# Moving the loads and splits of the token sums at sample's changes of stage, and starting sample's groups of heads later, in an encoder layer on one core

## The chip, the cores and the metric

The kernel runs on one core of a Trainium2 chip. The metric is the device time of one execution in microseconds (us). Three runs of the kernel before took 2102.96, 2103.63 and 2103.91 us, median 2103.63. A profile was taken of one more execution.

## The reference

Two sequences, prompt (512 tokens) and sample (1024 tokens), both 2048 wide, go through the same encoder layer:

```python
def mixer_layer(x, ...):
    h = rms_norm(x, norm_g)
    z = h @ w_in
    c_val, c_glu, c_gate, q, k, v, a_gate = jnp.split(z, split_points, axis=-1)
    q, k = apply_rope(q), apply_rope(k)
    conv_out = conformer_conv(c_val, c_glu, w_dw, b_dw, ln_g, ln_b, w_pw) * silu(c_gate)
    attn_out = banded_sink_attention(q, k, v, sink) * silu(a_gate)
    return x + concatenate([conv_out, attn_out]) @ w_out
```

`conformer_conv` is a gated linear unit, a depthwise convolution over 31 tokens, a layer norm and a product with `w_pw`. The attention has 8 heads in 2 groups (4 query heads share one key and value head), works in blocks of 128 tokens and looks one block to either side. A final RMS norm follows. Everything is in 32-bit floats.

## The kernel before

**Products.** Each 32-bit operand is split into an upper and a lower part (`parts`, lines 496 and 497: ACT makes the upper part, DVE subtracts for the lower; lines 499 and 500 do the same with a norm's factor; line 404 and 406 for the weights of prompt's jobs), and three matmuls (upper × upper, upper × lower, lower × upper) stand for one. The product of sample's tokens with `w_in` is done in the manner of Strassen and Winograd: a `Unit` (from line 93) makes a 2 × 2 block of the output from seven products instead of eight. Each of the seven (`product`, matmuls on line 199) is 12 matmuls of 128x128 by 128x512, 84 in a unit. Its operands are seven sums of weight tiles (`make0` to `make3`, line 141 subtracts) and seven sums of token tiles. When a product is done, `tap` (line 225, ACT) copies its PSUM bank out, and DVE adds it in (line 245). P1, P6, P7 and P4 share bank a, P5 and P3 bank c, P2 has b, so the next product of a bank waits for the tap.

**Token sums.** The seven sums of a half of the depth (in the order A11, A12, S2, S1, S3, S4, A22) stay in SBUF as split tiles (pool T1, 28 tiles, just seven sums of four tiles) for a whole stage. Four of them were computed once and written to memory (`sum_S`), the other three are plain tiles of the tokens (`xT_s`). `load_sum` (line 838, DMA issue on line 853) fetches one sum of four tiles on the queue of SP: steps 0 and 3 into the p tiles, the others into two A tiles (pool A has 4, p has 4). `token_sum` (line 777) splits them.

**Stages.** Sample's product runs in four stages: a plain block and 7 units, then 8 units for the convolution's channels on the other half of the depth, then 14 and 14 for the rest. The first two units of the second and fourth stage run interleaved, as a side pair. Between stages the token sums change; `switch` (line 1878, called at lines 1905 and 1906 for sample and a third time for the later product with `w_out`) hangs loads and splits onto the products of the last unit of the old stage and the first of the new: the loads of steps 0, 1 and 2 go ahead of the last unit, and after product n of it the sum of step n − 1 is split and the sum of step n + 2 loaded, since a sum is no longer needed once its product is done.

**After that.** 44 jobs of 48 matmuls (line 645) multiply prompt's tokens with `w_in`, 16 jobs with `w_pw` follow (line 337 and 1781 are plain products too), then units (`Onto`) for the product with `w_out` of both sequences, whose results DVE adds from PSUM (line 292).

**The order of the work.** The matmuls' order is written out by hand. Beside them run lanes (`Lane`, line 63), queues of generators for the small work: `conv` (depthwise convolution, lines 976, 1005 and 1013; L1039 to L1042 and L949 make the rotated and gated parts), `prep` (sums and norms: the squares of sample's rows are on line 873, a small chain of DVE turns them into factors, L712 puts them on diagonals and the matmul of L717 spreads them), and `attn` (attention). With every three matmuls a lane earns 3 × 216 ns times its rate, and a generator that yields a cost pauses until that much has been earned. So a cost of `rate * 4000` is 4 us of matmul time. `attend` (in `encoder`) puts the two groups of sample's heads into the lane `attn` at the start of prompt's jobs, with rate 1.8. `group` (line 1087) loads keys, values and the first queries, waits, splits them, and then does block by block `attention` (line 1112): scores (L1129), mask, maximum and sum (L1132), exponentials (L1143), transposes (L1163) and the product with the values (L1158).

The place in the program is not yet the place on an engine. A scheduler puts the instructions of every engine in order, by readiness and priority; an instruction that is ready, and whose tile is free, can be ahead of others that the program has before it. DMAs are issued by SP (its queue has most loads and stores) and a few by POOL.

Of the kernel before, what the change touches and what calls it, by code (L numbers as in the profile page):

```python
# [720 lines left out]
class Sequence:  # L721
# [365 lines left out]
    def group(self, g):  # L1087

        e, nc = self.e, self.e.nc
        if self.s == 0:  # L1090
            k, v = ([e.T1([self.T]) for _ in range(2)] for _ in range(2))
        else:
            kv = e.F([2, self.T], F32R), e.F([2, self.T], F32R)
            k, v = [(t[:, 0], t[:, 1]) for t in kv]
        held = []
        for src in (self.k_d[g], self.v_d[g]):
            held.append(e.A([self.T], F32))
            nc.sync.dma_start(held[-1], src)
        self.load_query(g, 0)
        yield e.attn.rate * LEAD  # L1100
        for dst in (k, v):
            e.parts(dst[0], dst[1], held.pop(0))
            yield 3500
        for b in range(self.B):
            yield from self.attention(g, b, k, v)

# [697 lines left out]
def encoder(ctx, tc, a):  # L1804
    e = Encoder(ctx, tc, a)
    sample, prompt = Sequence(e, 0), Sequence(e, 1)
# [9 lines left out]
    stages = [  # L1816
        [plain] + [u(0, False) for u in conv[1:]],
        [u(1, True) for u in conv],
        [u(1, False) for u in rest],
        [u(0, True) for u in rest],  # L1820
    ]
# [53 lines left out]
        u.order = TURNS  # L1875
    plain.before.append(first)

    def switch(unit, nxt, g, seq):

        held = {}  # L1880

        roomy = seq is sample

        def load(step):
            held[step] = seq.load_sum(SUMS[ALONE[step]], g, step % 3 or roomy and step == 6)

        def follow(step):
            for j, x in enumerate(held.pop(step)):
                seq.token_sum(SUMS[ALONE[step]], g, j, x)
            if step < 4 - roomy:  # L1890
                load(step + 3)
            elif step == 4 and roomy:
                load(6)

        def begin():
            load(0)
            load(1)
            load(2)

        unit.before.append(begin)  # L1900
        for step in range(7):
            u, at = (unit, step + 1) if step < 6 else (nxt, 0)
            u.after.setdefault(at, []).append(lambda step=step: follow(step))

    switch(stages[0][-1], stages[1][0], 1, sample)
    switch(stages[2][-1], stages[3][0], 0, sample)

    def pace(unit, rate, lane=e.conv):
        unit.before.append(lambda: setattr(lane, "rate", rate))
# [70 lines left out]
    def prepare():  # L1980
        until(lambda: sample.convolved == NC, e.conv)
        for half in halves:
            e.prep.add(half.prepare())
        e.prep.add(halves[0].fetch())
        e.attn.add(mix.attention_sums())
        for group in prompt.groups:
            e.attn.add(group)
# [29 lines left out]
    over[0][0].after[3] = [lambda: mix.put(6)]  # L2017
    over[0][-1].before += [e.prep.drain, e.attn.drain]
    switch(over[0][-1], over[1][0], 0, mix)

    def norm_last():
# [25 lines left out]
    at = len(e.preps)  # L2047
# [58 lines left out]
```

## Time and profile before

| | |
|---|---|
| median of three runs | 2103.63 us |
| profiled execution | 2106.77 us |
| its span in the profile | 2104.9 us |
| TensorE (PE) busy | 2067.4 us, 9250 matmuls |
| VectorE (DVE) busy | 1751.4 us |
| ScalarE (ACT) busy | 1042.5 us |
| DMA | 494.53 MB, 235 GB/s on average |

A row of the timeline has the start in us, the duration, engine, line (L199 is line 199 of the kernel before), operation, written and read tile, shape and count; in brackets the idle time of the engine ahead of it and what ended that. In the list of waits stand the matmul that waited, the instruction that released it, the total in us, the number of such waits and the longest. In the table by windows stand start and end, length, then busy time and count of PE, PEld (weights loaded into the array), DVE, ACT and POOL, then the granted clock of TensorE as a share of full speed, the share of the DMA engines in use, and GB/s. Matmuls overlap a little, so a run of them is read from the starts: 24 of 128x512 take 5.44 us, 0.2267 each.

### The profile page before, as it was taken

To read this page: it belongs to the slowest core of one execution; us is meant where nothing else is said; L and a number is where in the kernel's file an instruction comes from. 1 tells how busy PE (TensorE), PEld (TensorE's weight loads), DVE (VectorE), ACT (ScalarE), POOL (GpSimd) and SP (SyncE) were. 2 spreads that over 40 slices of the span, in tenths; PEclk is the share of its full clock that TensorE was granted. 3 is DMA by queue.
4 is the path that set the end of the run, shared out by engine and by line. 5 is a ranking of instruction groups with operands and counts; after the bars stand their busy time and mean duration, and the time that the engine had idled before them with its cause. 6 is when DMAs were issued, how large, how long until landed. Compare 5 with 4: busy or idle time off the path is not lost. (4 is left out here: it accounts for less than half of the span.)

```text
span 2104.9 us, 26942 instructions
## 1 busy us (share of the span) xinstructions
PE 2067.4 (98%) x9250; PEld 1696.0 (81%) x9250; DVE 1751.4 (83%) x2851; ACT 1042.5 (50%) x1685; POOL 77.3 (4%) x92
## 2 busy tenths in 40 slices
PE   9999999999999999999999999999999999999997
PEld 7878888888877887778888888887878788888886
DVE  8758798998889999999556877776799988898876
ACT  6476435333454443544456777336553343455444
POOL 0001110000002111100000000000000000000000
PEclk9999999999999999999999999999999999999999
DMA  7988887865577776955456565996689898678998
GB/s 265 322 290 247 203 217 226 295 201 172 181 228 193 172 170 170 270 162 163 156 170 190 169 187 180 315 332 223 233 276 305 269 321 295 207 251 272 299 323 276
DMA packets 247449, 494.53 MB, mean 235 GB/s; under 512 B 23184, under 2 KB 83984, under 8 KB 247312
## 3 DMA queue, kind: packets, MB, share of 16 engines
q1 hardware_dynamic: 234640, 469.74, 67.4%
q0 software_dynamic: 12672, 23.07, 6.9%
q8 instruction: 72, 1.18, 0.2%
q14 instruction: 65, 0.53, 0.1%
HBM read 331.77 MB, written 160.96 MB: 234 GB/s over the span
## 5 line engine op out<-in xcount | busy, mean ns | idle before, releaser
L199 PE MATMUL a<-t,hl 128*128 128x512 f32 x2640 | 633.4, 390 | 10.0 <-ACT u L225 4.8
L199 PEld LDWEIGHTS a<-t,hl 128*128 128x128 f32 x2640 | 493.2, 188 | 118.4 <-ACT u L225 8.1
L496 ACT ACTIVATE hl<-raw 128x1024 fp32r<-128x1024 f32 (+3 forms) x360 | 324.6, 902 | 435.6 <-DVE raw L141 96.3
L497 DVE TENSOR_TENSOR hl<-raw,hl 128x1024 fp32r<-128x1024 f32 (+3 forms) x360 | 370.1, 1028 | 152.6 <-ACT hl L496 148.7
L645 PE MATMUL a<-t,hl 128*128 128x512 f32 x1344 | 329.4, 395 | 0.5 <-DVE hl L497 0.5
L199 PE MATMUL c<-t,hl 128*128 128x512 f32 x1320 | 320.1, 390 | 3.1 <-DVE u L292 2.0
L199 PEld LDWEIGHTS c<-t,hl 128*128 128x128 f32 x1320 | 247.0, 188 | 56.6 <-DVE u L292 3.4
L645 PEld LDWEIGHTS a<-t,hl 128*128 128x128 f32 x1344 | 249.2, 189 | 51.4 <-DVE hl L497 1.0
L1013 DVE SCALAR_TENSOR_TENSOR f<-f,c_w_dw,f 128x512 f32<-128x512 f32 x248 | 175.3, 748 | 0.3
L645 PE MATMUL c<-t,hl 128*128 128x512 f32 x672 | 165.4, 394 | 0.0
L976 DVE SCALAR_TENSOR_TENSOR f<-f,c_w_dw,f 128x512 f32<-128x512 f32 x232 | 163.7, 746 | 1.8 <-ACT f L971 1.8
L645 PE MATMUL b<-t,hl 128*128 128x512 f32 x672 | 163.4, 392 | 0.2 <-DVE hl L497 0.2
L199 PE MATMUL b<-t,hl 128*128 128x512 f32 x660 | 160.2, 390 | 0.0
L645 PEld LDWEIGHTS b<-t,hl 128*128 128x128 f32 x672 | 124.9, 188 | 25.3 <-DVE hl L497 0.7
L645 PEld LDWEIGHTS c<-t,hl 128*128 128x128 f32 x672 | 125.1, 189 | 24.4
L199 PEld LDWEIGHTS b<-t,hl 128*128 128x128 f32 x660 | 123.7, 188 | 25.5
L1005 DVE SCALAR_TENSOR_TENSOR f<-f,w_both,f 128x512 f32<-128x512 f32 x120 | 89.8, 749 | 1.8
L225 ACT ACTIVATE u<-a 128x512 f32<-128x512 f32 x82 | 48.6, 592 | 56.5 <-PE a L199 53.7
L404 ACT ACTIVATE hl<-raw 128x1024 fp32r<-128x1024 f32 x44 | 46.4, 1056 | 60.5 <-PE a L645 22.3
L225 ACT ACTIVATE g<-a 128x512 f32<-128x512 f32 x78 | 46.3, 593 | 56.3 <-PE a L199 52.7
L1143 ACT ACTIVATE p<-p,tiny 128x384 f32<-128x384 f32 (+1 forms) x96 | 54.6, 570 | 38.4 <-DVE tiny L1140 28.1
L496 ACT ACTIVATE a<-pt 128x512 fp32r<-128x512 f32 x64 | 38.0, 593 | 68.6 <-PE pt L1163 68.2
(333 smaller groups left out, 2575.5 us busy)
## 6 DMA issues: line engine op xcount, KB each, us to landing
raw<-w_in SPq DMA_DIRECT2D x171, 512.0 KB, 5.1
raw<-wsum_P SPq DMA_DIRECT2D x32, 512.0 KB, 5.2
raw<-w_out SPq DMA_DIRECT2D x31, 512.0 KB, 5.4
raw<-w_pw SPq DMA_DIRECT2D x24, 512.0 KB, 4.4
raw<-w_last SPq DMA_DIRECT2D x24, 512.0 KB, 5.2
wsum_P<-raw SPq DMA_DIRECT2D x47, 256.0 KB, 3.5
f<-x_s SPq DMA_DIRECT2D x16, 512.0 KB, 7.2
a<-sum_S SPq DMA_DIRECT2D x24, 256.0 KB, 6.0
```

Source lines behind the costliest of these rows:

```text
L199: nc.tensor.matmul(acc, hl[:, l, o, j, :], toks[j][:, r], start=name in FRESH and j == 0 and q == 0, stop=name in LAST and j == HALF - 1 a ...
L225: nc.scalar.activation(t, bank, AF.Copy)
L404: e.nc.scalar.activation(t[:, 0], raw, AF.Copy)
L496: nc.scalar.activation(hi, x, AF.Copy)
L497: nc.vector.tensor_tensor(lo, x, hi.bitcast(F32), ALU.subtract)
L645: nc.tensor.matmul(job.acc[0], hl[:, l, kk // HALF, kk % HALF, :], r, start=i == 0 and p == 0, stop=i == nk - 1 and p == 2,)
L976: nc.vector.scalar_tensor_tensor(t, h[:, j : j + T], w(j), t, ALU.mult, ALU.add)
L1005: nc.vector.scalar_tensor_tensor(m0, odd[:, j : j + H], both(j), m0, ALU.mult, ALU.add)
L1013: nc.vector.scalar_tensor_tensor(out, d[:, j : j + H], w(2 * j + k), out if j else m0, ALU.mult, ALU.add)
L1143: nc.scalar.activation(p[:, 0:n], p[:, 0:n], AF.Exp, bias=nm[:, h : h + 1], accum_out=l[:, h : h + 1])
```

## The change

Three things, the first two for sample's two switches alone (`roomy`):

1. The loads of steps 1 and 2 are issued ahead of the unit before the last of the old stage, not of the last; the load of step 0 stays where it was.
2. The sum of step 3, 4 and 5 is split one product later, that of step 6 two products later: after products 1, 2, 3, 5 and 6 of the last unit and 0 and 2 of the next, where it was 1 to 6 and 0. The loads that follow a split go with it (that of step 6 comes after the split of step 4).
3. Each of sample's two groups of heads yields `e.attn.rate * 4000` between the split of its keys and values and its first block of attention.

The third switch and prompt's groups keep their order in the program.

```diff
@@ group @@
             yield 3500
+        if self.s == 0:
+            yield e.attn.rate * 4000
         for b in range(self.B):
             yield from self.attention(g, b, k, v)
@@ encoder @@
-    def switch(unit, nxt, g, seq):
+    def switch(unit, nxt, g, seq, early=None):
...
-        def begin():
-            load(0)
-            load(1)
-            load(2)
-
-        unit.before.append(begin)
-        for step in range(7):
-            u, at = (unit, step + 1) if step < 6 else (nxt, 0)
+        if early:
+            early.before.append(lambda: (load(1), load(2)))
+            unit.before.append(lambda: load(0))
+        else:
+            unit.before.append(lambda: (load(0), load(1), load(2)))
+        for step, at in enumerate((1, 2, 3, 5, 6, 7, 9) if roomy else (1, 2, 3, 4, 5, 6, 7)):
+            u, at = (unit, at) if at < 7 else (nxt, at - 7)
             u.after.setdefault(at, []).append(lambda step=step: follow(step))
 
-    switch(stages[0][-1], stages[1][0], 1, sample)
-    switch(stages[2][-1], stages[3][0], 0, sample)
+    switch(stages[0][-1], stages[1][0], 1, sample, stages[0][-2])
+    switch(stages[2][-1], stages[3][0], 0, sample, stages[2][-2])
```

## The prediction

> **What bounds the kernel now.** I read the share of each engine first, then what TensorE waited for, then the stretches around those waits.
>
> ```profile
> span 2104.9 us, 26942 instructions
> PE 2067.4 (98%) x9250; PEld 1696.0 (81%) x9250; DVE 1751.4 (83%) x2851; ACT 1042.5 (50%) x1685; POOL 77.3 (4%) x92
> ```
>
> The span is 2104.9 us, and TensorE (PE) is busy in 98% of it. Neither the number nor the shape of its matmuls changes, so the time can move only through the 37.5 us in which PE stands still (2104.9 − 2067.4) and through its clock. What ends those waits (us in total, times, longest):
>
> ```profile
> engine line waited for: us in total, times, longest us
> PE a L199 <- ACT u L225: 4.8, 6, 1.3
> PE s L1129 <- DVE tiny L1132: 2.5, 1, 2.5
> PE s L1129 <- ACT a L496: 2.3, 1, 2.3
> PE c L199 <- DVE u L292: 2.0, 1, 2.0
> PE a L199 <- DVE hl L497: 1.8, 1, 1.8
> PE s L717 <- DVE u L712: 1.2, 1, 1.2
> PE s L199 <- ACT hl L496: 1.1, 1, 1.1
> ```
>
> No wait is longer than 2.5 us and no line costs 5. The waits for L225 are taps of a product (a PSUM bank copied out), those for L496 and L497 are halves of a split, those for L1132 and L712 attention and norm work on DVE. So the change is a matter of a few such waits; the order of the engines' instructions, which can be read from both programs, decides which.
>
> **Part 1, loads of the token sums moved one unit forward.** The scheduler issues a load when its tile is free, not where the code has it. For the second of sample's switches the issues of the A tiles are already these:
>
> ```profile
> L853 SPq DMA_DIRECT2D a<-xT_s x12: 327/424/679, 180.8 to 611.4; - x12
> L853 SPq DMA_DIRECT2D a<-sum_S x12: 320/426/646, 190.2 to 596.0; - x12
> ```
>
> The first are issued at 180.8 and 190.2 us; the last, for the seventh sum, at 611.4. One unit is 84 matmuls, some 19 us; the loads that the edit moves already go out hundreds of us ahead, and their places on SP's queue are the same in both programs. At the first switch only two sum_S tiles move, seven places ahead on SP, past five loads of x_s, and one square of a row norm (L873) goes later on ACT. I cost the loads themselves at nothing; what hides them is the earlier issue, and if that were lost a tile would land about a load late, where ACT already waits.
>
> **Part 2, splits one product later.** The same scheduler undoes most of this: the splits of steps 3, 4 and 5 stand in nearly the same order on ACT and DVE. What moves is small work around them, in three places.
>
> *First switch.*
>
> ```profile
> 146.03 5.73 PE L199 MATMUL a<-t,hl 128*128 128x512 f32 x24 [1.19 <-ACT g L225]
> 153.66 0.50 PE L717 MATMUL s<-u,ones_r 128*128 128x512 f32 x1 [1.22 <-DVE u L712]
> 168.84 3.47 PE L199 MATMUL a<-t,hl 128*128 128x512 f32 x14 [0.89 <-ACT u L225]
> ...
> 153.13 0.47 DVE L712 TENSOR_SCALAR u<-c_ident,tinyr 128x128 fp32r<-128x128 f32 x2
> 155.94 1.41 DVE L500 SCALAR_TENSOR_TENSOR t<-p,c_norm_g,t 128x512 fp32r<-128x512 f32 x2
> 157.27 0.69 DVE L245 TENSOR_TENSOR g<-b,g 128x512 f32<-128x512 f32 x1
> 157.87 0.68 DVE L497 TENSOR_TENSOR hl<-raw,hl 128x512 fp32r<-128x512 f32 x1
> ```
>
> The first gap stays: the tap behind it still stands after a square of x_s. The spread matmuls (L717) go 24 matmuls later, 24 × 0.227 = 5.44 us (5.73 us for 24 here, whose last end is modelled), so the 1.22 goes. But on DVE five splits of L500, the add L245 and the split L497 now stand ahead of L712's matrices: 5 × 0.70 + 0.60 + 0.60 = 4.7 us by starts, and ACT has to make the upper halves first, so L712 is some 7 us later, and L717 waits 1.4 to 2.2 (I take 1.8). The tap behind the gap at 168.84 now stands ahead of a split of L499, so that 0.89 goes. Sum: 1.8 − 1.22 − 0.89 = **−0.3**, from −1.0 to +1.7.
>
> *Second switch.*
>
> ```profile
> 899.71 5.47 DVE L1005 SCALAR_TENSOR_TENSOR f<-f,w_both,f 128x512 f32<-128x512 f32 x7
> ```
>
> Two depthwise steps on DVE (L1005, 5.47 / 7 = 0.78 each) come between the splits of the second-last sum. Its A tile is free up to 1.6 us later, then the last load, then the split behind PE's 1.1 us on L496. I count a third of it, since PE's wait ends on ACT, which runs ahead of its own needs there: **+0.5**, from −0.7 to +1.3.
>
> *Third stage, side pair just over.*
>
> ```profile
> 663.86 2.73 DVE L1013 SCALAR_TENSOR_TENSOR f<-f,c_w_dw,f 128x512 f32<-128x512 f32 x4
> 666.60 0.69 DVE L1039 TENSOR_TENSOR u<-g,f 64x512 f32<-64x512 f32 x1
> 667.30 0.69 DVE L1040 TENSOR_TENSOR u<-g,f 64x512 f32<-64x512 f32 x1
> 668.02 1.23 DVE L497 TENSOR_TENSOR hl<-raw,hl 128x1024 fp32r<-128x1024 f32 x1
> 669.16 0.68 DVE L1041 TENSOR_TENSOR g<-g,f 128x512 f32<-128x512 f32 x1
> ...
> 669.30 1.66 PE L199 MATMUL a<-t,hl 128*128 128x512 f32 x6 [1.82 <-DVE hl L497]
> 671.91 3.02 PE L199 MATMUL c<-t,hl 128*128 128x512 f32 x12 [0.95 <-ACT g L225]
> ```
>
> DVE runs without a pause here, and PE waits 1.82 for the split that starts at 668.02. In the changed order one L1013 and L1041 stand ahead of it: 0.67 + 0.60 = 1.27 later, so the wait is 3.1. The next wait, 0.95 behind a tap and a store, shrinks by about as much. Alone that is +0.4. A wait of 3.1 has a second price, from the clock (next).
>
> **Part 3, sample's groups of heads 4 us of lane time later.**
>
> ```profile
> 882.66 0.68 DVE L497 TENSOR_TENSOR a<-u,a 128x512 fp32r<-128x512 f32 x1
> 896.50 0.48 DVE L1132 CUSTOM_DVE_ANT_0 p<-s,c_mask,c_attn_sink 128x256 f32<-128x256 f32 x1
> ...
> 885.32 5.97 PE L645 MATMUL a<-t,hl 128*128 128x512 f32 x25 [0.53 <-DVE hl L497]
> 891.85 2.69 PE L645 MATMUL a<-t,hl 128*128 128x512 f32 x11
> 897.04 1.41 PE L1129 MATMUL s<-t,a 128*128 128x256 f32 x6 [2.49 <-DVE tiny L1132]
> ```
>
> ```profile
> 896.00:898.00 2.00, 0.96 (x5) 0.96 (x6) 2.00 (x7) 1.39 (x2) 0.00 (x0) 0.86 0.60 205
> 898.00:900.00 2.00, 2.00 (x8) 1.61 (x7) 1.97 (x9) 0.24 (x1) 0.00 (x0) 0.50 0.78 223
> 900.00:902.00 2.00, 2.00 (x9) 1.59 (x8) 1.93 (x3) 1.98 (x10) 0.00 (x0) 0.79 0.04 14
> 1428.00:1430.00 2.00, 1.99 (x12) 1.66 (x13) 1.57 (x7) 0.00 (x0) 0.00 (x0) 1.00 0.88 323
> ```
>
> The last three numbers are granted clock, DMA share and GB/s. After the 2.49 us wait the clock drops: 2 × (0.14 + 0.50 + 0.21) = 1.7 us of work lost. After the wait of 2.3 at 1428 it stays 1.00. So here the clock's price begins between 2.3 and 2.5.
>
> [...]
>
> In the changed program the first scores come after 45 matmuls of their job instead of 27 (18 × 0.227 = 4.1 us later), the second after 6 more instead of 11. The query split (882.66) leaves the place ahead of the weight split, so the 0.53 goes, and stands behind the later weight split, so the third score matmul waits for it: PE would be there at 891.3 + 4.1 − 0.5 = 894.9; the weight split ended at 896.5, where L1132 starts, less 1.2 that DVE and ACT gain ahead of it, plus 0.6 for the query split, is 895.9, so about 1.1 with the start of the group. Three of L1005 then stand ahead of L1132, so the second scores wait some 0.6 again. No wait reaches 2.3, so the clock holds: 1.1 + 0.6 − 0.53 − 2.49 − 1.7 = **−3.0**, from −4.5 to +0.5.
>
> Back to 669: 3.1 is past 2.49, so I charge the clock at 7 in 10, 0.7 × 1.7 = 1.2, in all **+1.6**, from −0.4 to +3.
>
> Later, prompt's groups begin at the same matmul as before, so the 2.3 wait at 1428 stays, but their blocks end 36 matmuls (8 us) later, and the last passes deeper into the product with w_out. There two waits cost 2.0 + 0.5:
>
> ```profile
> 1645.92 0.96 PE L199 MATMUL c<-t,hl 128*128 128x512 f32 x3 [2.02 <-DVE u L292]
> 1647.65 0.73 PE L1158 MATMUL pv<-a,f 128*128 128x512 f32 x2 [0.53 <-DVE a L497]
> 1640.00:1660.00 20.00, 17.45 (x82) 13.76 (x81) 17.36 (x27) 6.08 (x9) 0.00 (x0) 1.00 0.76 254
> ```
>
> Counting DVE's instructions ahead of each weight split, the changed order has as often less as more there (up to 6 us either way); bounded by losing these waits (−2.5) and having them twice (+2.5), I take **+0.5**.
>
> **Sum**: −0.3 + 0.5 + 1.6 − 3.0 + 0.5 = −0.7 us. The profiled execution took 2106.77 us (the span and 1.87 around it), 3.1 above the median of the runs, 2103.63; I carry the difference over to the median: **2102.9 us**.
>
> **The rivals.**
>
> - *The clock holds and the later heads relieve the DVE* (faster): the wait at 669 stays under the point where the clock drops (−1.2 on my sum), the prompt start gains its full 4.5 (−1.5), and the waits at 1645 go (−3.0 from my +0.5). For it: those two clock-priced places are the dearest in the trace. Against: DVE is still full at 1645. −0.7 − 5.7: 2097.2.
> - *The heads fall into the full DVE* (slower): each attention block that moves on behind 1580 us repeats the pair 2.0 + 0.5 (+2.0 on my sum), and one of its waits, or that at 1428, which is already 2.3, passes 2.5 and halves the clock (+1.7), while 669 pays its whole 1.7 + 0.4 (+0.5). It decides as soon as two tenths of a us are added to the 2.3. Against: prompt's first scores stand at the same matmul. −0.7 + 4.2 + the wait's own growth of 1: 2108.1.
> - *It doesn't do what it says*: the scheduler hoists loads and splits as before, and only the lane's 4 us is left, given back when the lane is drained at the last w_out unit: 2103.6.
>
> **How the numbers follow.** A measurement of this kernel can tell about 0.2%, 4.2 us, from no change. The forecast, 0.40: bounds −4.5 to +4, nearly all inside 0.2% (faster 0.05, same 0.30, slower 0.05). The faster rival 0.27 (faster 0.26, same 0.01). The slower rival 0.27 (slower 0.25, same 0.02). Nothing moves, 0.06 (same 0.04, one hundredth either side). Together faster 0.32, same 0.37, slower 0.31. The forecast's own range is 2099.2 to 2107.6; with the rivals, 2095.5 to 2110.0.
>
> **What would show it.** PE's waits after the change: no 2.5 for L1132 near 897 and a clock of 1.00 there; a wait of about 3 for L497 near 669, with or without half clock behind it; L717 waiting about 1.8 near 158; the same loads of xT_s and sum_S at 180 to 190 us. I am wrong if the waits of prompt's heads, past 1400, add up to over 4 us more or less than now, or if a wait appears that is not in this list.

## The result, and the profile after

22 runs of each, side by side, gave a median of 2105.60 us for the changed kernel against 2102.44 before: ratio 1.0016, 95% interval [1.0008, 1.0023], that is +3.4 us (+1.7 to +4.8) by the ratio. The sign is clear, the size below the 0.2% that the prediction took as its bound. The forecast was −0.7 us. That 2105.60 lies inside the forecast's range, 2099.2 to 2107.6, is owed to the width of the range: the sum went the other way.

The two profiled executions say the opposite: the span after is shorter. The runs before go from 2094.28 to 2110.69 us, so one execution tells nothing about 3 us; the profile before was a long one (2106.77).

```profile
span 2103.6 us, 26958 instructions
PE 2066.0 (98%) x9250; PEld 1696.7 (81%) x9250; DVE 1751.8 (83%) x2851; ACT 1043.3 (50%) x1685; POOL 77.2 (4%) x92
```

PE is busy 2066.0 us where it was 2067.4; the same work, the same idle sum. What differs is the list of PE's waits after:

```profile
engine line waited for: us in total, times, longest us
PE s L1783 <- ACT hl L496: 3.3, 1, 3.3
PE a L199 <- ACT u L225: 2.8, 5, 1.0
PE a L199 <- DVE hl L497: 2.6, 2, 2.1
PE s L1131 <- ACT a L496: 2.3, 1, 2.3
...
PE s L717 <- DVE u L712: 1.4, 1, 1.4
PE s L1131 <- DVE tiny L1134: 1.3, 2, 0.8
...
PE s L1131 <- DVE a L497: 1.0, 1, 1.0
```

(Lines from 1104 on count two more than before.) The wait of 2.5 for the row maxima is gone, L717 waits 1.4, as the steps said. The longest wait, 3.3 at 2060 us, says little of the change: at that place each of the 15 profiles that the section on the prediction compares has a wait, of 1.5 to 3.3 us, and the time from the third change of token sums to the last product is 328.9 us on average with sample's heads late and 328.8 without. The timeline of PE at the start of prompt's jobs and at its first scores:

```profile
891.36 0.74 PE L1131 MATMUL s<-t,a 128*128 128x256 f32 x4 [0.95 <-DVE a L497]
...
894.01 1.02 PE L1131 MATMUL s<-t,a 128*128 128x256 f32 x6 [0.50 <-DVE tiny L1134]
...
909.61 0.33 PE L1165 MATMUL pt<-c_ident,p 128*128 128x128 f32 x1 [0.67 <-ACT p L1152]
```

and further on in the same timeline

```profile
1074.76 1.03 PE L1131 MATMUL s<-t,a 128*128 128x256 f32 x6 [0.83 <-DVE tiny L1134]
```

0.95 and 0.50 stand where 1.1 and 0.6 were forecast. The waits of 0.67 and 0.83 were in no list: transposes that now come before their exponentials are ready, and a later block's second scores.

Windows with the granted clock (third number from the right):

```profile
892.00:894.00 2.00, 1.51 (x7) 0.88 (x6) 1.96 (x5) 1.15 (x2) 0.00 (x0) 1.00 0.78 202
1420.00:1422.00 2.00, 0.26 (x1) 0.26 (x2) 1.83 (x4) 0.63 (x1) 0.00 (x0) 0.91 0.83 240
1422.00:1424.00 2.00, 2.00 (x8) 1.81 (x9) 0.46 (x3) 0.00 (x0) 0.00 (x0) 0.50 0.86 326
1424.00:1426.00 2.00, 2.00 (x12) 1.77 (x11) 1.14 (x5) 0.00 (x0) 0.00 (x0) 0.74 0.02 6
```

The clock now holds near 893, and is halved behind prompt's first scores, after a wait of 2.28 us; before, a wait of 2.26 at that place left it at 1.00:

```profile
1428.01 0.74 PE L1129 MATMUL s<-f,a 128*128 128x256 f32 x4 [2.26 <-ACT a L496]
```

And between matmul 6830 and 6960 (matmuls of the products alone, those of lines 199, 337, 645 and 1781, 8364 of the 9250, counted from 0), at the third change of token sums, there are four waits, where PE had this one before:

```profile
1749.94 2.60 PE L199 MATMUL s<-t,hl 128*128 128x512 f32 x10 [0.37 <-DVE hl L497]
```

After:

```profile
1723.86 0.73 PE L199 MATMUL a<-t,hl 128*128 128x512 f32 x2 [0.78 <-ACT hl L496]
1725.12 0.97 PE L199 MATMUL a<-t,hl 128*128 128x512 f32 x3 [0.52 <-DVE hl L497]
1726.56 3.02 PE L199 MATMUL c<-t,hl 128*128 128x512 f32 x12 [0.47 <-DVE u L292]
...
1746.78 3.02 PE L199 MATMUL a<-t,hl 128*128 128x512 f32 x12 [1.34 <-DVE u L292]
```

### The profile page after: what moved, and what is told of

Its sections match the earlier page's. It is cut to its first block, busy times and chain, and to the rows that moved or that the text cites. A ratio compares the mean times of both kernels' runs of the same rounds, so it can differ in the third digit from the quotient of the medians.

```text
span 2103.6 us, 26958 instructions
## 1 busy us (share of the span) xinstructions
PE 2066.0 (98%) x9250; PEld 1696.7 (81%) x9250; DVE 1751.8 (83%) x2851; ACT 1043.3 (50%) x1685; POOL 77.2 (4%) x92
## 5 line engine op out<-in xcount | busy, mean ns | idle before, releaser
L1013 DVE SCALAR_TENSOR_TENSOR f<-f,c_w_dw,f 128x512 f32<-128x512 f32 x248 | 175.9, 753 | 0.4
```

What stands on the lines that cost most here:

```text
L1013: nc.vector.scalar_tensor_tensor(out, d[:, j : j + H], w(2 * j + k), out if j else m0, ALU.mult, ALU.add)
```

## The experiments

Since one execution scatters by some us, two things were measured for each kernel: its ratio to the kernel before on the same chip (every ratio below is to that kernel, and the us are of 2102), and in its profile the time between the starts of fixed matmuls. The three parts of the change turn out to be separate in the engines' orders: part 1 alone changes only the first switch, part 2 only the second switch and the start of the third stage, part 3 nothing ahead of 884 us.

### The three parts, one by one

```diff
 # p1_loads (on the changed kernel, without the yield in group)
-        for step, at in enumerate((1, 2, 3, 5, 6, 7, 9) if roomy else (1, 2, 3, 4, 5, 6, 7)):
+        for step, at in enumerate((1, 2, 3, 4, 5, 6, 7)):
 # p2_splits (on the changed kernel, without the yield in group)
-    switch(stages[0][-1], stages[1][0], 1, sample, stages[0][-2])
-    switch(stages[2][-1], stages[3][0], 0, sample, stages[2][-2])
+    switch(stages[0][-1], stages[1][0], 1, sample)
+    switch(stages[2][-1], stages[3][0], 0, sample)
 # p3_heads (on the kernel before)
+        if self.s == 0:
+            yield e.attn.rate * 4000
```

> Part 1 alone (loads of steps 1 and 2 a unit earlier); on every engine only the first switch differs from the kernel before. By the terms of the prediction: -0.3 us against before (-1.0 to +1.7), with the waits at 146 and 153 us replaced by one of about 1.4 to 1.8 for L712. If this part is where the 3 us come from, +3. If the difference comes from the heads, within 1 us of before.

> Part 2 alone (splits one or two products later); only the second switch and the start of the third stage differ from before. By the prediction +2.1 us (0.5 at the switch, 1.6 at the wait for L497 near 669, with the clock halved behind it in most runs). The profile of the changed kernel has that wait at 2.12 and the clock at 1.00, so without the clock term: +0.5 to +0.9.

> Part 3 alone (sample's groups 4 us later); everything up to 884 us is as before, everything from there to about 1700 us is as in the changed kernel. By the prediction -2.5 us (-3.0 at the prompt start, +0.5 later). Rival: what the start gains is given back and more, at prompt's first scores (2.3 us, with the clock halved) and in the product with w_out: +2 to +5 us, and the profile shows PE ahead of before's at matmul 3909 and behind it by the last unit.

> The changed kernel once more, for a second profile and as the yardstick of the three parts on the same chip: +3 us against before by the result (ratio 1.0016). If the parts add up, the three single parts sum to this within 1.5 us. The place of each wait in the second profile tells which losses are of the program and which of the single execution; the clock is expected to halve behind prompt's first scores if that belongs to the program.

Measured: part 1 0.9991 [0.9978, 1.0003] (−1.9 us), part 2 1.0007 [0.9995, 1.0019] (+1.5), part 3 1.0009 [0.9996, 1.0021] (+1.9), all three again 1.0014 [1.0004, 1.0025] (+2.9). The parts sum to +1.5, inside the intervals. Part 3 does not gain what the prediction has it gain. In the profile of `a2_again` the clock stays at 1.00 behind prompt's first scores, after a wait of 2.51 us, so the halving there does not belong to every execution.

### Part 3 cut in two

The delay of part 3 works at two places: sample's own heads come later (early half), and so, since the lane `attn` is one queue, do all heads and sums behind them (late half). A negative cost gives lane time back, so each can be had alone:

```diff
 # early_half (on part 3)            # late_half (on before)
         for b in range(self.B):             for b in range(self.B):
             yield from ...                      yield from ...
+        if self.s == 0 and g == 1:  +        if self.s == 0 and g == 1:
+            yield -e.attn.rate * 8000 +          yield e.attn.rate * 8000
```

> The early half of part 3: sample's groups wait 4 us each as in part 3, and 8 us of lane time are given back behind the second group, so that every engine's order is that of part 3 up to prompt's heads and that of before from there on. By the prediction's term for the prompt start: -3.0 us against before. Rival, from the six profiles so far (main matmul 3756 to 5712 took 538.5 to 540.4 us with before's order and 538.3 to 539.3 with part 3's, the longest one with a halved clock): -1 to +1, since the wait of 2.5 us is replaced by several that sum to as much. Matmuls 6830 to 6960 should take 29.5 to 30.3 us as with before's order, not 32.3 to 33.8.

> The late half of part 3: sample's groups start as before, and 8 us of lane time are yielded behind the second group, so that the order is before's up to prompt's heads and that of part 3 from there on. By the prediction's term (+0.5): within 1.5 us of before. Rival, the loss lies here: +3 to +5, of which some 3 us between matmul 6830 and 6960 (the third change of token sums, at 1725 to 1755 us) and 1 to 2 between 5712 and 6740.

> The kernel before once more, for a second profile on this chip: no difference from itself (within 2 us). If the halved clock behind the wait near 897 is of the program, it is there again; if it depends on where the wait falls in the clock's own rhythm, the wait of 2.5 us is there again and the clock may stay at 1.00, and the span is nearer to 2098 than to 2104.9.

> Part 1 and the early half of part 3 together, without part 2 and without the late half. If the parts add up: part 1's -2 us (ratio 0.9991 alone) and the early half's -1 to +1, so -3 to -1 against before, and below the changed kernel by 4 to 6. By the prediction's terms: -0.3 and -3.0, so -3.3.

Measured: early half 1.0021 [1.0007, 1.0034] (+4.4 us), late half 1.0008 [0.9992, 1.0024] (+1.7), before against itself 0.9995 [0.9981, 1.0009], part 1 with the early half 1.0006 [0.9994, 1.0017] (+1.3, where −3 to −1 was expected). So my term of −3.0 is refuted by the early half alone: its interval, +1.5 to +7, lies on the other side. The rival's −1 to +1 missed it as well, because its figure covered only the matmuls up to 5712: the wait behind them is longer too. The timeline of PE in `early_half`:

```profile
1409.35 9.46 PE L645 MATMUL a<-t,hl 128*128 128x512 f32 x41
1421.54 1.22 PE L1133 MATMUL s<-f,a 128*128 128x256 f32 x4 [2.73 <-ACT a L496]
```

and on SP's queue, in the same kernel,

```profile
1410.75 0.84 SPq L490 DMA_DIRECT2D msum_S<-u  x1
1411.64 0.59 SPq L490 DMA_DIRECT2D msum_S<-g  x1
1412.28 0.72 SPq L1098 DMA_DIRECT2D a<-k_d  x1
```

while PE and then SP's queue in `b2_again`, with before's order, have

```profile
1408.59 9.46 PE L645 MATMUL a<-t,hl 128*128 128x512 f32 x41
1419.24 0.74 PE L1129 MATMUL s<-f,a 128*128 128x256 f32 x4 [1.20 <-ACT a L496]
```

and

```profile
1409.57 0.42 SPq L490 DMA_DIRECT2D msum_S<-g  x1
1410.05 0.42 SPq L1098 DMA_DIRECT2D a<-k_d  x1
```

Prompt's keys are asked for 1412.28 − 1409.35 = 2.9 us after the job's first matmul instead of 1.5: SP's queue has them right behind two stores of token sums for the product with `w_out` (`msum_S`), where `b2_again` has one; that these come later because the lane is later is argued. The scores wait 2.73 instead of 1.20. (Over the 15 profiles without the moved load of the next section: 2.28 to 3.57 with the early half, 1.20 to 2.26 without. The keys are asked for 2.5 to 3.9 us after the job's first matmul with it, 1.0 to 2.8 without, and over all 15 this time and the wait go together, with a correlation of 0.92.)

`b2_again` has the same second scores as the profile before, with a wait of 1.88 and the clock at 1.00 behind it:

```profile
890.86 1.03 PE L1129 MATMUL s<-t,a 128*128 128x256 f32 x6 [1.88 <-DVE tiny L1132]
```

and in the table by windows

```profile
891.00:893.00 2.00, 2.00 (x12) 1.78 (x13) 2.00 (x8) 0.23 (x1) 0.00 (x0) 1.00 0.79 217
```

Other profiles with before's order have a wait of 2.45 to 2.49 there; of the ten profiles with that order the clock is halved in two (behind 2.49 in the profile before and 2.45 in `q_p1`).

### The query load, and the last block

```diff
 # q_before, q_after, q_p1: queries between keys and values
             nc.sync.dma_start(held[-1], src)
+            if len(held) == 1:
+                self.load_query(g, 0)
-        self.load_query(g, 0)
 # late_last (on late_half), after_last (on the changed kernel)
         for b in range(self.B):
+            if self.s == 1 and g == 1 and b == self.B - 1:
+                yield -e.attn.rate * 8000
             yield from self.attention(g, b, k, v)
```

> The kernel before with one load moved: the first queries of a group are loaded between its keys and its values, not behind both. If prompt's first scores wait for the query load's place on SP's queue (released by the split of the queries on ACT, 1.2 to 2.3 us in the profiles with before's order), that wait falls by the landing of one load, to 0 to 1.5, and the time by about 1 us. If they wait for the keys' split instead, no change.

> The changed kernel with the same load moved. Its wait at prompt's first scores was 2.3 and 2.5 us, in kernels with its early half 2.7 to 3.6, four times in five with the clock halved behind it. If the late query load causes both, the wait falls below 1.6, the clock stays at 1.00 there, and the time falls by 2 to 3 us against the changed kernel, to within 1.5 us of before. If the early half's cost is elsewhere, it stays at +3.

> The late half of part 3 with its 8 us given back ahead of prompt's very last block of heads, so that only the blocks in between are late. If the 2.5 to 3.5 us between matmul 6830 and 6960 come from the last block's lateness, by the order it leaves on SP at the third change of token sums, that stretch takes 29.5 to 30.3 us again, and the whole is within 1.5 us of before. If they come from the time that DVE is behind, it stays at 32 to 34.

> Part 1 alone with the query load moved: the candidate for a kernel faster than both. Part 1 alone measured 0.9991 [0.9978, 1.0003], the moved load about -1 us by theory: -2 to -4 us against before. If part 1's gain was chance (its stretch, matmul 480 to 690, shows -0.4 us in the profiles), -1 to -2.

Measured: 1.0003 [0.9987, 1.0019] for the load moved on before, 1.0024 [1.001, 1.0037] on the changed kernel, 0.9988 [0.9972, 1.0003] on part 1, 1.0009 [0.9997, 1.0021] for `late_last`. No gain from moving the load is shown, and the wait stays (2.41 in `q_before`). PE's timeline in `q_after`:

```profile
1411.25 7.55 PE L645 MATMUL a<-t,hl 128*128 128x512 f32 x32 [0.82 <-DVE hl L497]
1421.86 1.22 PE L1132 MATMUL s<-f,a 128*128 128x256 f32 x4 [3.07 <-ACT a L496]
```

With the queries asked for earlier, the scheduler put the scores behind 2 + 32 matmuls of their job, not 41, so PE comes sooner to the same wait. My expectation took the order on PE as fixed. That the place of the key loads on SP sets this wait is read from the traces (the correlation above), not shown by a run.

`late_last` answers the other question: matmul 6830 to 6960 takes 30.05 us, where `late_half` took 32.60. The lateness of the one last block of heads does it.

### Inside the changed kernel

```diff
 # after_back (on the changed kernel)
         for b in range(self.B):
             yield from self.attention(g, b, k, v)
+        if self.s == 0 and g == 1:
+            yield -e.attn.rate * 8000
 # p12 (on the changed kernel)
-        if self.s == 0:
-            yield e.attn.rate * 4000
```

So `after_back` has parts 1, 2 and the early half, and `p1_again` is `p1_loads` once more.

> Parts 1 and 2 without part 3. By the stretches of the profiles: -0.4 us at the first switch, +1.0 at the second and the third stage, so +0.6 against before (-1 to +2). If part 3 carries the loss, this is 2 to 4 us below the changed kernel. [...]

> The changed kernel with 8 us of lane time given back ahead of prompt's last block of heads. If the third change of token sums costs 3 us because of that block alone, matmul 6830 to 6960 takes 29.5 to 30.3 us and the whole is 2.5 to 3.5 us below the changed kernel, so within 1.5 us of before. If the loss lies in the early half, +2 to +3 against before. [...]

> The changed kernel with 8 us of lane time given back behind sample's groups: parts 1, 2 and the early half. If the early half is the dearer one (ratio 1.0021 alone), this stays at +3 to +5 against before, with a wait of 2.3 to 3.6 us at prompt's first scores. If the late half is, within 2 us of before. [...]

> Part 1 alone, once more, on another lot of runs. If its 0.9991 was a gain, -1 to -3 us against before; if it was chance, -1 to +1, as its stretch in the profiles (matmul 480 to 690) says. [...]

Measured: `p12` 1.0004 [0.9991, 1.0016] (+0.8 us), `after_last` 1.0001 [0.9989, 1.0013] (+0.2), `after_back` 1.0017 [1.0003, 1.0031] (+3.6), `p1_again` 0.9997 [0.9986, 1.0008] (−0.6). Without part 3 the loss is mostly gone (+0.8 in `p12`). With the early half it is there in `after_back`, but not in `after_last`, which has the early half too. The stretch at the third change of sums is smooth again in `after_last`:

```profile
1720.25 2.88 PE L199 MATMUL a<-t,hl 128*128 128x512 f32 x12
1722.97 2.88 PE L199 MATMUL c<-t,hl 128*128 128x512 f32 x12
1725.69 5.60 PE L199 MATMUL a<-t,hl 128*128 128x512 f32 x24
```

It took 30.46 us there, and 30.69 in `after_back`. But the runs don't agree on what that is worth as a whole: `after_back` should then be low too, and `late_last` below `late_half`, and they are not.

A least-squares fit, weighted by the intervals, of one number per factor to the ratios of all kernels but those with the moved load (14, as us of 2102) gives part 1 −1.2 ± 1.4, part 2 +1.3 ± 1.6, the early half +2.3 ± 1.6, the blocks in between −0.2 ± 1.9, the last block +0.8 ± 2.2 (95%; rough, as kernels of one batch share the runs of before).

No version is clearly faster than the kernel before. Part 1 with the moved load is the lowest (0.9988, its interval reaches 1.0003), and part 1 alone, −1.9 at first, was −0.6 when it was run again.

## Why the prediction was wrong

The mean of a stretch in profiles with the order in question against those without it (those with the moved load left out), beside the term of the prediction:

| matmuls | what differs | without | with | difference | predicted |
|---|---|---|---|---|---|
| 480 to 690 | part 1 | 53.3 (7) | 52.6 (8) | −0.7 | −0.3 |
| 2500 to 2900 | part 2 | 97.1 (9) | 98.4 (6) | +1.3 | +2.1 |
| 3756 to 5712 | early half | 538.7 (8) | 538.8 (7) | 0.0 | −3.0 |
| 5712 to 5775 | early half | 23.3 (8) | 24.6 (7) | +1.3 | 0 |
| 5775 to 6740 | either half | 254.9 (6) | 255.4 (9) | +0.6 | +0.5 |
| 6830 to 6960 | last block late | 30.4 (11) | 33.0 (4) | +2.6 | 0 |

Single profiles scatter by 1 us or more in each; the sum of +5.1 lies just above the measured +1.7 to +4.8. The border at 5775 does not part the two rows beside it cleanly: where the late half is in, 32 matmuls of attention stand between 5712 and 5775, else 38, and the six score matmuls that change sides take 0.80 us in `b2_again`. Taken as one, 5712 to 6740 is 278.2 us without part 3 (6 profiles), 278.4 with the late half alone (2), 281.2 with the early half alone (3) and 279.3 with both (4). So the late blocks themselves cost nothing that shows there; the early half does.

- **Part 1**: the size was right, the place in the working was not. The loads of the second switch keep their place, as I said. But the −0.3 at the first switch, which I booked under the later splits of part 2, comes from the moved loads: `p1_loads` has another order there and L717 waiting 1.7, and `p2_splits` has before's order. L717 waits 1.4 after (I took 1.8), and the stretch gives −0.7.
- **Part 2** was right in sign and place. The wait near 669 did not grow by 1.27 but by 0.3, to 2.1. DVE's timeline after does have L1013 and L1041 ahead of the split:

```profile
657.80 2.74 DVE L1013 SCALAR_TENSOR_TENSOR f<-f,c_w_dw,f 128x512 f32<-128x512 f32 x4
...
661.97 0.75 DVE L1013 SCALAR_TENSOR_TENSOR f<-f,c_w_dw,f 128x512 f32<-128x512 f32 x1
662.64 0.69 DVE L1041 TENSOR_TENSOR g<-g,f 128x512 f32<-128x512 f32 x1
663.25 1.22 DVE L497 TENSOR_TENSOR hl<-raw,hl 128x1024 fp32r<-128x1024 f32 x1
```

and PE's has

```profile
659.61 2.79 PE L199 MATMUL a<-t,hl 128*128 128x512 f32 x11
664.52 1.66 PE L199 MATMUL a<-t,hl 128*128 128x512 f32 x6 [2.12 <-DVE hl L497]
```

where PE's timeline before had

```profile
664.68 2.79 PE L199 MATMUL a<-t,hl 128*128 128x512 f32 x11
```

The four L1013 start 659.61 − 657.80 = 1.81 us ahead of PE's eleven matmuls, where they started 664.68 − 663.86 = 0.82 ahead before. PE had lost 1.0 us at 634 to a tap, which the wait I added had in reserve. I took the time between two engines as it was in one execution. The 1.2 for the clock was not paid either: none of the six profiles with part 2 has a halved clock behind this wait (`p2_splits` has one behind the tap at 636, after 3.41 us), and four of the nine without it do, after waits of 1.81 to 1.86.

- **Part 3, the prompt start** (−3.0) is the step that failed. Its waits were forecast to a tenth or two, yet it gained nothing, for two reasons. 1.7 of the 3.0 was the halved clock, which was taken from the one profile as a property of the program; it is there in two of the ten profiles with before's order. And the other 1.3 came back as waits that the sum did not look for, further along the same chain (0.67 at the transposes, 0.83 at 1074).
- **Prompt's first scores**: that they "stand at the same matmul" was right, and the conclusion "so the 2.3 wait at 1428 stays" was wrong. The same place on PE does not keep the loads' place on SP. The slower rival had named this wait, and that its clock could tip; in the profiles with the early half it tipped in six of seven, against two of eight without.
- **The third change of sums** was not in the list: I looked at the waits at 1645 us and not at the change of sums behind them. On SP the loads of the third sum's four p tiles were one run of 2.28 us:

```profile
1720.07 2.28 SPq L853 DMA_DIRECT2D p<-msum_S  x4
```

After, they go out as two and two, a weight load and a store between:

```profile
1712.89 1.13 SPq L853 DMA_DIRECT2D p<-msum_S  x2
1716.09 0.32 SPq L490 DMA_DIRECT2D part_out<-u  x1
1716.69 0.33 SPq L126 DMA_DIRECT2D raw<-w_out  x1
1717.08 1.31 SPq L853 DMA_DIRECT2D p<-msum_S  x2
```

On ACT the weight split of the next product stands behind the splits of those tiles, and PE waits for it. But only two of the four profiles with a late last block have that wait. What all four have, and none of the other eleven, is two waits for DVE's additions from PSUM (L292), 0.47 to 1.29 and 1.01 to 1.34 us, in `late_half` for example

```profile
1723.35 3.04 PE L199 MATMUL c<-t,hl 128*128 128x512 f32 x12 [1.29 <-DVE u L292]
1743.31 3.04 PE L199 MATMUL a<-t,hl 128*128 128x512 f32 x12 [1.06 <-DVE u L292]
```

Shown is that giving the last block its old place removes them; what makes these additions late stays open.

- **The list of waits** that the prediction reads before left out a wait as long as its longest, without a mark:

```profile
PE s L1781 <- DVE f L1675: 2.5, 1, 2.5
```

Behind it the clock was halved as well (0.50 from 2061.39 to 2064.80 us), so the wait near 897 was not the only one with that price.

The rival "it doesn't do what it says" was right for parts 1 and 2 as far as the loads of the second switch and the splits go, and wrong for part 3.

## What to carry to other kernels

Where a chain is moved to dodge one wait, add up the whole stretch up to the next point where both orders meet, in several profiles: here waits of 0.53 and 2.49 became four that sum to 2.95. When a lane is one queue, a delay at its front is a delay for all behind it, and its price is paid at the queue's last item, 800 us later. And a term that comes from the clock belongs into the sum with the share of executions that have it, not with its size in one.

## What the runs showed of the hardware

The clock's record in the trace of the kernel before shows 0.50 from 897.44 and from 2061.39 us, that of the changed kernel from 1421.65 and from 2059.94, each time for 3.413 us (and once more behind PE's last matmul, for 8.1 and 8.2). The two starts lie 1163.95 us apart before and 638.29 after, which is 341 and 187 times 3.413 us to within 0.04. Counted in stretches of 3.413 us forward and back from these starts, PE stood idle for 2.49, 2.49, 2.18 and 3.18 us in the four stretches right ahead of a halved one, and for at most 1.50 in any other between its first and last matmul. The wait of 2.26 before, at 1428.01, lies in two stretches, 0.76 and 1.50, and that of 2.12 after, at 664.52, with 1.49 and 0.63; the clock stayed at 1.00 behind both. Of the 2.28 at 1421.74 after, 2.18 lie in one, and the clock was halved. These two profiles don't show where between 1.50 and 2.18 the clock tips, nor whether it is so in other executions.

The length of a wait alone doesn't tell it: behind a wait of 1.83 in `p1_loads`

```profile
665.85 2.80 PE L199 MATMUL a<-t,hl 128*128 128x512 f32 x6 [1.83 <-DVE hl L497]
```

the clock was halved, as the windows show,

```profile
666.00:668.00 2.00, 2.00 (x5) 1.55 (x6) 2.00 (x4) 0.60 (x1) 0.00 (x0) 0.50 0.06 20
```

while behind 2.51 in `a2_again` and 1.88 in `b2_again` it stayed at 1.00. My threshold "between 2.3 and 2.5" was the chance of one execution. A halved stretch costs 1.7 us, half of its 3.413: in `p1_early` the twelve matmuls behind a wait of 2.00 take 4.45 us from start to start (864.44 to 868.89), where twelve just before take 2.72 (856.83 to 859.55). `p1_early` has three such stretches, behind waits of 1.86, 2.00 and 3.57, so by my estimate 3 × 1.7 = 5 us of the 16 us by which runs of the kernel before differ (2094.28 to 2110.69) can come from this.
